# A transformer layer on eight cores: new assumed delays, banks, buffers and places of small work in a statically scheduled kernel

## Chip, cores, metric

One Trainium2 chip, all eight cores running the same program on different tokens. The time is device microseconds of the slowest core. Fast runs are compared with fast runs; a run in which one die shows a lower granted tensor-engine clock is left out (2058.0 us in one run of the changed kernel, with cores 0 to 3 at 0.825 to 0.838 and the others at 0.997).

## The reference, cut

```python
def hybrid_layer(x, c, ...):                       # x (1, 8192, 2048), c (1, 2048), f32
    mod = jax.nn.silu(c) @ w_ada + b_ada           # six vectors of 2048: conditioning
    shift_m, scale_m, gate_m, shift_f, scale_f, gate_f = split(mod, 6)
    h = rms_norm(x, g_pre_mix) * (1.0 + scale_m) + shift_m
    u, v, p, ga, gb = split(h @ w_in, ...)         # 2048, 2048, 1024, 2048, 2048 columns
    y_a = spatial_gating(gelu(u), gelu(v), ...) @ w_branch_a
    y_b = multiscale_pool(p, w_pool, pool_scale) @ w_branch_b
    merged = sigmoid(ga) * y_a + sigmoid(gb) * y_b
    x = x + gate_m * rms_norm(merged @ w_out, g_post_mix)
    h = rms_norm(x, g_pre_ffn) * (1.0 + scale_f) + shift_f
    a, g = split(causal_depthwise_conv(h @ w_up, conv_w, conv_b), 2)   # 2 x 5632
    return x + gate_f * rms_norm((gelu(a) * g) @ w_down, g_post_ffn)
```

Each core handles 1024 tokens plus a halo, feature-major, mostly in float16 with float32 PSUM.

## The kernel before, where the change touches it

The kernel records every operation, then orders each engine's queue at build time with a cost model. The queues are written in that order, so a wrong cost becomes a wrong place in a queue.

```python
# the model's idea of when an operation ends
if o.dma:
    free[e] = t + (1100.0 if e == "pool" else 80.0)
    pipe = max(pipe, t + 1000.0) + o.cost          # bytes / 335, in ns
    o.end = pipe + 1200.0
else:
    free[e] = t + o.cost
    o.end = t + o.cost + o.lat
...
def dot(self, out, in0, in1, accum, soon):         # one conditioning value per partition, on DVE
    ...
    if soon:
        o.at = self.npe + 60                       # due 60 matmuls from here
```

The conditioning vectors are dot products on the vector engine, of 128 weight rows at a time, streamed through small buffers beside other work:

```python
mtile = [view(SC, i * 4096, 4096, H16, 1) for i in range(3)]
def mod_next(upto, ntile):
    while mdone[0] < upto:
        while mdone[0] - mdone[1] >= ntile:
            mod_dot_next()                         # frees a buffer: POOL's next load waits for it
        ...
        S.dma("pool", t[:, 0, :], w_adaT[r:r + 128, :], writes=[t])
...
def g_step():                                      # once per pair of gate-stage weight tiles
    g_next()                                       # next 1 MB of w_gab
    npairs[0] += 1
    n = npairs[0]
    mod_next(3 + n * 3 // 2 if n <= 12 else min(len(mf), n + 9), 3 if n <= 12 else 1)
    if n in (19, 21):
        load("o%d" % (n // 20), (RD, n // 20 * 16384), *specs["o%d" % (n // 20)])
```

The start of branch B, where the last pooling blocks are evicted:

```python
for eb, at in ((0, y0), (1, 3072)):
    S.act(qv[6 + eb][:, 0:1024], ps[:, at:at + 1024], AF.Identity, scale=col(vec, V_PS + eb))
...
state["slot"] += 1                                 # output block 1 takes the banks of block 0
yb_mms(0, b0, range(6, 8))
```

The second norm reads residual rows through six buffers while w_up is being loaded:

```python
xs2 = [...2 in SC...] + [...4 in RC...]
for j in {9: (1, 2), 11: (0, 3), 15: (4,)}.get(i, ()):
    load_up((0, 0, j), PL[j])
```

## Time and profile before

| | before |
|---|---|
| median of the 5 runs | 1787.31 us (1784.23 to 1817.48) |
| spans of the cores in the profiled run | 1772.0 to 1784.7 us |
| tensor engine busy, slowest core | 1682.8 us, 94% |
| waits of the tensor engine after its first main matmul, mean of the cores | 24.9 us |
| stretches at half clock between there and the end, mean per core (20 of the 22 last 3.41 us, two last 6.83) | 2.8 |
| after the last matmul | 13.9 us |

PE stands for the matmuls of the tensor engine, PEld for its weight loads, DVE for the vector engine, ACT for the scalar engine; POOL and SP issue the loads. w_gab are the weights of the gate stage. An eviction copies a result out of a PSUM bank; a matmul that takes the same bank waits for it (1.27 us at 159.7 us on core 3 of the kernel before). "First main matmul" is the 241st of the tensor engine, the first of the pooling projection, at about 80 us. A row of the waits view names the engine that sat idle, whose result ended the wait, the total, the number of waits and the longest. A timeline row gives start, duration, engine, operation and tiles, and in brackets the idle time before it and what ended it. Almost every compute row has one of a few source lines, those of the helpers that record it, so one goes by the tiles: in SC<-SC,xlo 128x1152 a weight tile is multiplied with the conditioning vector in xlo.

### The profile page before, as it was taken

What the parts mean: (1) busy time and instruction counts of PE and PEld (TensorE: products, weight loads), DVE (VectorE), ACT (ScalarE), POOL (GpSimd) and SP (SyncE); (2) the same over time, 40 slices, a digit from 0 to 9 for tenths busy, and PEclk for the clock granted to TensorE, in tenths of its full rate; (3) what the DMA queues carried; (4) which work ended last, traced back from release to release, by engine and by line L of the source; (5) the groups of instructions that cost most, each with busy time, mean ns of one, the idle gap of its engine ahead of it and who ended that gap; (6) DMA issues with size and microseconds to landing.
All of it is one profiled execution on the core that took longest, in us unless ns stands there. A gap on an engine that the chain in (4) does not pass through costs nothing.

```text
span 1784.7 us, 32368 instructions; the slowest of 8 cores (1772.0 to 1784.7 us)
## 1 busy us (share of the span) xinstructions
PE 1682.8 (94%) x12892; PEld 1226.1 (69%) x12892; DVE 1186.0 (66%) x1664; ACT 663.6 (37%) x980; POOL 125.9 (7%) x194
## 2 busy tenths in 40 slices
PE   4399999999999999999989999999999999999996
PEld 1265544566788888877568885588854887488876
DVE  0566614464778668750667998467987678967968
ACT  5115522511233332122768542255410442035475
POOL 0100100000011010100000000000000000100100
PEclk9999999999999999999999999999999999999998
DMA  9998999933799976994797544545435553555496
GB/s 247 165 169 145 150 170 153 151 66 62 123 164 157 159 133 128 150 164 67 184 213 169 97 84 71 95 84 95 83 59 97 94 88 53 98 95 95 68 226 227
DMA packets 85160, 227.42 MB, mean 127 GB/s; under 512 B 5650, under 2 KB 34706, under 8 KB 84499
## 3 DMA queue, kind: packets, MB, share of 16 engines
q0 software_dynamic: 54368, 178.79, 60.6%
q1 hardware_dynamic: 30644, 46.56, 8.6%
q8 instruction: 104, 1.70, 0.4%
q14 instruction: 44, 0.36, 0.1%
HBM read 387.34 MB, written 16.78 MB: 226 GB/s over the span
## 4 chain that ended last, share of the span: by engine, by line
PE 68%; DMA 19%; DVE 7%; issue 3%; ACT 1%; SPq 1%; POOL 0%; DVEq 0%; ACTq 0%; POOLq 0%
PE ps L311 68%; DMA R<-w_adaT 5%; DMA SC<-w_adaT 5%; DMA RING<-w_adaT 3%; DMA RD<-w_sA 2%; DVE R L340 2%; DMA RC<-xT 1%; DMA R<-xT 1%; DVE R L323 1%; DVE SC L335 1%; DVE RING L340 1%; DMA RING<-w_down 1%; SPq L355 1%; DVE SC L340 1%; DVE SC L323 1%
## 5 line engine op out<-in xcount | busy, mean ns | idle before, releaser
L311 PE MATMUL ps<-RD,RING 128*128 128x257 f16 (+2 forms) x5172 | 654.0, 283 | 7.0 <-ACT SC L318 3.1
L311 PEld LDWEIGHTS ps<-RD,RING 128*128 128x128 f16 x5172 | 504.0, 98 | 128.6 <-issue 9.4
L318 ACT ACTIVATE R<-ps 128x514 f32<-128x514 f32 (+4 forms) x222 | 140.3, 633 | 563.5 <-PE ps L311 544.0
L311 PE MATMUL ps<-RC,RING 128*128 128x257 f16 (+6 forms) x2168 | 347.1, 313 | 0.3 <-DMA RING<-w_down 0.2
L311 PEld LDWEIGHTS ps<-RC,RING 128*128 128x128 f16 x2168 | 207.4, 98 | 118.0 <-issue 1.9
L335 DVE SCALAR_TENSOR_TENSOR SC<-SC,vec 128x1024 f32<-128x1024 f32 (+1 forms) x188 | 218.3, 1178 | 14.1 <-ACT SC L318 7.6
L323 DVE TENSOR_TENSOR RING<-RING 128x1024 f16<-128x1024 f16 (+2 forms) x250 | 157.7, 640 | 26.5 <-PE ps L311 18.8
L323 DVE TENSOR_TENSOR SC<-ps,R 128x514 f32<-128x514 f32 x144 | 99.5, 691 | 88.3 <-PE ps L311 75.9
L311 PE MATMUL ps<-RING 128*128 128x257 f16 x1248 | 146.5, 274 | 0.0
L323 DVE TENSOR_TENSOR R<-ps,R 128x512 f32<-128x512 f32 (+4 forms) x174 | 104.4, 613 | 46.3 <-PE ps L311 44.2
L311 PEld LDWEIGHTS ps<-RING 128*128 128x128 f16 x1248 | 122.1, 98 | 18.0
L311 PE MATMUL ps<-SC,RING 128*128 128x342 f16 (+1 forms) x654 | 125.5, 341 | 5.6 <-ACT RC L318 3.7
L311 PE MATMUL ps<-RING,RD 128*128 128x512 f16 x576 | 125.1, 379 | 1.3 <-ACT R L318 0.7
L318 ACT ACTIVATE SC<-SC,vec 128x1024 f32<-128x1024 f32 (+1 forms) x94 | 108.4, 1158 | 38.8 <-DVE SC L323 27.8
L318 ACT ACTIVATE SC<-ps 128x514 f32<-128x514 f32 (+1 forms) x89 | 55.8, 627 | 137.8 <-PE ps L311 137.6
L311 PEld LDWEIGHTS ps<-SC,RING 128*128 128x128 f16 x654 | 63.9, 98 | 59.3 <-issue 8.6
L311 PEld LDWEIGHTS ps<-RING,RD 128*128 128x128 f16 x576 | 56.2, 98 | 69.6 <-issue 2.2
L311 PE MATMUL ps<-R 128*128 128x257 f16 x816 | 96.5, 274 | 2.7 <-DVE SC L323 2.7
L311 PE MATMUL ps<-R,RING 128*128 128x257 f16 x816 | 96.2, 274 | 1.2 <-ACT R L318 0.8
L318 ACT ACTIVATE RD<-ps 128x514 f32<-128x514 f32 (+2 forms) x77 | 45.7, 593 | 123.5 <-PE ps L311 123.4
L311 PEld LDWEIGHTS ps<-R 128*128 128x128 f16 x816 | 79.8, 98 | 14.9 <-issue 3.4
L311 PEld LDWEIGHTS ps<-R,RING 128*128 128x128 f16 x816 | 79.5, 98 | 13.2 <-issue 1.7
(142 smaller groups left out, 1454.8 us busy)
## 6 DMA issues: line engine op xcount, KB each, us to landing
RING<-w_up POOLq DMA_DIRECT2D x44, 1024.0 KB, 8.0
RING<-w_gab POOLq DMA_DIRECT2D x24, 1024.0 KB, 9.7
SC<-w_adaT POOLq DMA_DIRECT2D x32, 512.0 KB, 11.8
RING<-w_in POOLq DMA_DIRECT2D x7, 2048.0 KB, 22.5
R<-w_adaT POOLq DMA_DIRECT2D x6, 2048.0 KB, 18.9
RING<-w_down POOLq DMA_DIRECT2D x16, 768.0 KB, 6.7
RING<-w_down POOLq DMA_DIRECT2D x14, 640.0 KB, 6.2
R<-xT SPq DMA_DIRECT2D x15, 576.0 KB, 16.4
```

The costliest lines, as they stand in the source:

```text
L311: return self.op("pe", lambda e: e.matmul(out, lhsT=lhsT, rhs=rhs, start=start, stop=stop, skip_group_check=resume), [lhsT, rhs], [out], s ...
L318: return self.op("act", lambda e: e.activation(out=out, in_=in_, func=func, bias=bias, scale=scale, accum_out=accum), self._aps(in_, scale ...
L323: return self.op(eng, lambda e: e.tensor_tensor(out=out, in0=in0, in1=in1, op=op), [in0, in1], [out], cost=65.0 + per * self._n(out))
L335: return self.op("dve", lambda e: e.scalar_tensor_tensor(out=out, in0=in0, scalar=s, in1=in1, op0=op0, op1=op1), self._aps(in0, s, in1), [ ...
L340: o = self.op("dve", lambda e: e.scalar_tensor_tensor(out=out, in0=in0, scalar=1.0, in1=in1, op0=ALU.mult, op1=ALU.mult, accum_out=accum), ...
L355: return self.op(eng, lambda e: e.dma_start(out=out, in_=in_), reads, writes, rtags, wtags, dma=True, cost=b / 335.0, after=after)
```

## The change

The intent: keep the tensor engine fed. The cost model gets an assumed lag for loads that arrive late and a later deadline for the dots; several blocks get other banks or buffers; eight of 32 conditioning tiles move to the output projection; projection blocks cover evictions; and the tail handles several blocks per instruction. The core of the diff, with cuts marked:

```diff
-                o.end = pipe + 1200.0
+                o.end = pipe + 1200.0 + o.lat
...
-            o.at = self.npe + 60
+            o.at = self.npe + soon                 # 60, and 180 for the gate stage's dots
...
 # lags: shift loads 2000, gm3 30000, gate-stage tiles 5000 (1000 for gf), second norm's residuals 3000
-            load("gm%d" % g, (R1, 16512), *specs["gm%d" % g])
+            load("gm%d" % g, (R1, 16512), *specs["gm%d" % g], lag=30000.0 if g == 3 else 0.0)
...
 # pairs of pooling blocks: the second trails by two steps
-            for kc in kcs:
-                fm_mms(b0, p_w(n), h_rhs, PCS_P, [kc], kcs[-1] + 1, kcs[0])
-                fm_mms(b1, p_w(n + 1), h_rhs, PCS_P, [kc], kcs[-1] + 1, kcs[0])
+            for i in range(len(kcs) + 2):
+                fm_mms(b0, p_w(n), h_rhs, PCS_P, kcs[i:i + 1], kcs[-1] + 1, kcs[0])
+                fm_mms(b1, p_w(n + 1), h_rhs, PCS_P, kcs[i - 2:i - 1] if i > 1 else (), kcs[-1] + 1, kcs[0])
...
-        for eb, at in ((0, y0), (1, 3072)):
-            S.act(qv[6 + eb][:, 0:1024], ps[:, at:at + 1024], AF.Identity, scale=col(vec, V_PS + eb))
         for eb in range(2):
             S.act(qv[6 + eb][:, 1024:1026], rest[...], ...)
-        state["slot"] += 1
+        for a in (0, 512):
+            S.act(qv[6][:, a:a + 512], ps[:, y0 + a:y0 + a + 512], AF.Identity, scale=col(vec, V_PS))
+            S.ts(qv[7][:, a:a + 512], ps[:, 3072 + a:3584 + a], col(vec, V_PS + 1), ALU.mult)
...
-                    for c in range(8):
+                    for c in (0, 1, 2, 6, 7, 3, 4, 5):
...
+        MG = 24
-            mod_next(3 + n * 3 // 2 if n <= 12 else min(len(mf), n + 9), 3 if n <= 12 else 1)
-            if n in (19, 21):
-                load("o%d" % (n // 20), ...)
+            mod_next(3 + n * 3 // 2 if n <= 12 else min(MG, n + 9), 3 if n <= 12 else 1)
+            if 18 <= n < 22:
+                i = (n - 18) // 2
+                load("o%d" % i, (RD, i * 16384), *specs["o%d" % i], 4, only=[n % 2 * 2, n % 2 * 2 + 1])
...
-        mod_next(3, 3)
-            g_plain("gb", QH, i // 4, i % 2, 1 - i // 2 % 2, (0, 2, 4)[i % 3])
+            g_plain("gb", QH, i // 4, i % 2, 1 - i // 2 % 2, (4, 0, 4, 2)[i])
...
-        g_pairs(gq[17:], QU, lambda: None)
+        g_pairs(gq[17:], QU, lambda: ox.append(out_cover()))   # 14 k-steps of output block 0
         ...
+        out_part(1, 2 - ox[0], range(14))
...
+        xs2 = 15 residual buffers instead of 6
-            for j in {9: (1, 2), 11: (0, 3), 15: (4,)}.get(i, ()):
+            for j in {9: (1,), 11: (0, 3)}.get(i, ()):          # j = 4 and 2 after the second norm
...
 # output projection, first half
+            if i % 2 == 0:
+                mod_next(MG + 1 + i // 2, 2)
...
 # first up blocks: 14 k-steps of two or three blocks interleaved, other banks
-                plain((1, 2, 0, 3, 4), 0, (0, 3, 6), False, ...)
+                plain((1, 0, 3, 4, 2), 0, (6, 3, 0), False, ...)
...
 # tail: blocks per eviction in the four token sets
+        groups = [[1] * 16, [2] * 8, [2] * 8, [4, 4, 4, 2, 2]]
```

More of the change, by code (lines that the diff above doesn't have):

```diff
@@ L351, in memset, with dma @@
         return self.op(eng, lambda e: e.memset(out, v), [], [out], cost=60.0 + 0.3 * self._n(out))
-    def dma(self, eng, out, in_, reads=(), writes=(), rtags=(), wtags=(), after=()):
+    def dma(self, eng, out, in_, reads=(), writes=(), rtags=(), wtags=(), after=(), lag=0.0):
         b = int(np.prod(in_.shape)) * (4 if in_.dtype == F32 else 2)
         return self.op(eng, lambda e: e.dma_start(out=out, in_=in_), reads, writes, rtags, wtags, dma=True, cost=b / 335.0,
-                       after=after)
+                       lat=lag, after=after)
 def build_program():
@@ L438, in piece_dst, with load @@
             return view(where[0], where[1], nk * ncols * 2, H16, nk)
-        def load(key, where, w, r0, nk, c0, ncols, parts=1, only=None, after=()):
+        def load(key, where, w, r0, nk, c0, ncols, parts=1, only=None, after=(), lag=0.0):
             dst = piece_dst(where, nk, ncols)
@@ L455, in load @@
                     src = w[(r0 + i * n) * 128:(r0 + (i + 1) * n) * 128, c0:c0 + ncols].rearrange("(k p) n -> p k n", p=128)
-                last = S.dma("pool", d, src, writes=[d], after=after)
+                last = S.dma("pool", d, src, writes=[d], after=after, lag=lag)
             loaded[key] = dst
@@ L498, in like, with rsqrt @@
             return v3(ap2, len(pieces))
-        def rsqrt(out, in_, scale):
-            S.act(out, in_, AF.Ln, scale=scale, bias=epst[:])
+        def rsqrt(out, in_, scale, table=True):
+            o = S.act(out, in_, AF.Ln, scale=scale, bias=epst[:])
+            if not table:
+                o.cost -= 1300.0
             S.act(out, out, AF.Exp, scale=-0.5)
@@ L519, in mod_c, with mod_dots @@
             return d
-        def mod_dots(key, f0, acc=None, soon=True):
+        def mod_dots(key, f0, acc=None, soon=60):
             w = loaded[key]
@@ L715, in shift_load @@
         def shift_load(i, after=()):
-            load("h%d" % i, (RING, 16384 + i % 3 * 4096), *specs["h%d" % i], after=after)
+            load("h%d" % i, (RING, 16384 + i % 3 * 4096), *specs["h%d" % i], after=after, lag=2000.0)
         def shift_add(i):
@@ L721, in shift_add @@
             o, sh = hT[:, i, :], mod_fm[:, i:i + 1]
-            S.tt(sh, col(macc, i), col(bada, i), ALU.add)
+            d = S.tt(sh, col(macc, i), col(bada, i), ALU.add)
             if i == 15:
                 S.stt(o, o, sh, ALU.add, xlo[:], ALU.add)
-            else:
-                S.act(o, xres[i], AF.Identity, scale=col(gs_m, i), bias=sh)
+            elif i % 2 == 0:
+                S.ts(o, xres[i], col(gs_m, i), ALU.mult, sh, ALU.add)
+            if i % 2 == 0 and i:
+                S.act(hT[:, i - 1, :], xres[i - 1], AF.Identity, scale=col(gs_m, i - 1), bias=mod_fm[:, i - 1:i], after=[d])
         for n in range(4, 8):
@@ L766, in build_program @@
                     shift_step(i)
-                load_next(0)
+                    if i == 6:
+                        load_next(0)
         load_next(2)
@@ L867, in build_program @@
         gst = [view(SC, 12304 + i * 2056, 2056, F32) for i in range(2)]
-        macc2 = view(SC, 16416, 128, F32)
+        macc2 = view(SC, 16528, 128, F32)
         merged = yb
@@ L891, in mod_dot_next @@
             mdone[1] += 1
-            mod_dots("%s.%d" % (sec, f), f, macc2 if sec == "gf" else None)
+            mod_dots("%s.%d" % (sec, f), f, macc2 if sec == "gf" else None, 180)
             if (sec, f) == ("sf", 15):
@@ L907, in mod_next @@
                 r = ((("hf", "sf", "gf").index(sec) + 2) * 16 + f) * 128
-                S.dma("pool", t[:, 0, :], w_adaT[r:r + 128, :], writes=[t])
+                S.dma("pool", t[:, 0, :], w_adaT[r:r + 128, :], writes=[t], lag=5000.0 if sec != "gf" else 1000.0)
                 loaded["%s.%d" % (sec, f)] = t
@@ L1013, in g_step @@
             n = npairs[0]
-            mod_next(3 + n * 3 // 2 if n <= 12 else min(len(mf), n + 9), 3 if n <= 12 else 1)
-            if n in (19, 21):
-                load("o%d" % (n // 20), (RD, n // 20 * 16384), *specs["o%d" % (n // 20)])
+            mod_next(3 + n * 3 // 2 if n <= 12 else min(MG, n + 9), 3 if n <= 12 else 1)
+            if 18 <= n < 22:
+                i = (n - 18) // 2
+                load("o%d" % i, (RD, i * 16384), *specs["o%d" % i], 4, only=[n % 2 * 2, n % 2 * 2 + 1])
         for i in range(3):
@@ L1030, in build_program, with out_cover, out_part @@
         g_step()
+        while mdone[1] < MG:
+            mod_dot_next()
         g_token_sums(QU)
-        g_pairs(gq[17:], QU, lambda: None)
-        while mdone[1] < len(mf):
-            mod_dot_next()
+        def out_cover():
+            x = 2 * (ng[0] % 2)
+            out_part(0, x, range(14))
+            return x
+        def out_part(blk, b0, kcs):
+            for kc in kcs:
+                for pi, (c0, n) in enumerate(PCS_1):
+                    S.mm(bank(b0 + pi)[:, 0:n], loaded["o0"][:, kc, blk * 128:(blk + 1) * 128], merged[:, kc, c0:c0 + n], kc == 0, kc == KC - 1)
+        ox = []
+        g_pairs(gq[17:], QU, lambda: ox.append(out_cover()))
         load("o2", (RING, 0), *specs["o2"])
         load("o3", (RING, 16384), *specs["o3"])
+        out_part(1, 2 - ox[0], range(14))
         mixT = view(R1, 0, 65664, F32, 16)
@@ L1041, in build_program, with out_block @@
         sqx = [view(R1, 65664 + i * 1156, 1156, BF16) for i in range(3)] + [view(RD, 32896, 1156, BF16)]
-        def out_block(blk, pieces):
+        def out_block(blk, pieces, b0=None):
             w = loaded["o%d" % (blk // 4)]
             c0, n = pieces[0][0], sum(m for _, m in pieces)
-            pv = fm_block(lambda kc: w[:, kc, (blk % 4) * 128:(blk % 4 + 1) * 128], lambda kc, a, m: merged[:, kc, a:a + m], pieces)
+            if b0 is not None:
+                out_part(blk, b0, range(14 if blk < 2 else 0, KC))
+                pv = bview(b0, pieces)
+            else:
+                pv = fm_block(lambda kc: w[:, kc, (blk % 4) * 128:(blk % 4 + 1) * 128], lambda kc, a, m: merged[:, kc, a:a + m], pieces)
             i = state["rr"] % len(sqm[n])
@@ L1056, in sum_mms, with rms @@
                 S.mm(bank(b0 + pi)[:, 0:n], ones_bf[:], sq[:, c0 - pieces[0][0]:c0 - pieces[0][0] + n], first, last, side=True)
-        def rms(b0, dst, pieces):
-            rsqrt(like(dst, pieces), bview(b0, pieces), 1.0 / D)
+        def rms(b0, dst, pieces, table=True):
+            rsqrt(like(dst, pieces), bview(b0, pieces), 1.0 / D, table)
         rs1, rs2 = view(SC, 0, 2312, F32), view(SC, 8224, 1792, F32)
@@ L1063, in build_program @@
         xs1 = [view(RING, 32768 + 2312 * i, 2312, F32) for i in range(7)] + [view(SC, 10016 + 2312 * i, 2312, F32) for i in range(2)]
-        xs2 = [view(SC, 10016 + 2312 * i, 1792, F32) for i in range(2)] + [view(RC, 24576 + 1792 * i, 1792, F32) for i in range(4)]
+        xs2 = ([view(SC, 10016 + 2312 * i, 1792, F32) for i in range(2)] + [view(SC, 14640, 1792, F32)] +
+               [view(RING, 40992 + 1792 * i, 1792, F32) for i in range(4)] + [view(RC, 24576 + 1792 * i, 1792, F32) for i in range(4)] +
+               [view(RING, 24576 + 1792 * i, 1792, F32) for i in range(4)])
         def norms(pieces, rs, xs, b0):
@@ L1071, in norms @@
                 m, x = mixT[:, i, c0:c0 + n], xs[i % len(xs)]
-                S.dma("sp", x, xT[i * 128:(i + 1) * 128, 126 + c0:126 + c0 + n], writes=[x])
+                S.dma("sp", x, xT[i * 128:(i + 1) * 128, 126 + c0:126 + c0 + n], writes=[x], lag=3000.0 if c0 else 0.0)
                 S.tt(m, m, rs, ALU.mult)
@@ L1138, in build_program @@
         fq += [("dn", (3, j)) for j in range(3)]
-        for i, blk in enumerate(range(16)):
-            sum_mms(6, out_block(blk, PCS_1), PCS_1, i == 0, i == 15)
+        state["slot"] = 0
+        for i in range(16):
+            sum_mms(6, out_block(i, PCS_1, (ox[0], 2 - ox[0], 4)[i] if i < 3 else None), PCS_1, i == 0, i == 15)
+            if i % 2 == 0:
+                mod_next(MG + 1 + i // 2, 2)
+        while mdone[1] < len(mf):
+            mod_dot_next()
         rms(6, rs1, PCS_1)
@@ L1239, in plain, with mms @@
             todo = [(j, m) for j in js for m in range(2)]
-            if t:
-                first = bufs[:3]
-                for kc in range(KC):
-                    for i, (j, m) in enumerate(todo[:3]):
-                        for pi in range(2):
-                            S.mm(bank(first[i] + pi)[:, 0:257], loaded[("up", 0, 0, j)][:, m, kc, :],
-                                 h2T[:, kc, t, pi * 257:(pi + 1) * 257], kc == 0, kc == KC - 1)
+            def mms(b0, j, m, kcs):
+                for kc in kcs:
+                    for pi in range(2):
+                        S.mm(bank(b0 + pi)[:, 0:257], loaded[("up", 0, 0, j)][:, m, kc, :],
+                             h2T[:, kc, t, pi * 257:(pi + 1) * 257], kc == 0, kc == KC - 1)
+            for kc in range(14):
+                for i, (j, m) in enumerate(todo[:2 + t]):
+                    mms(bufs[i], j, m, [kc])
             for i, (j, m) in enumerate(todo):
                 b0 = bufs[i % len(bufs)]
-                if not t or i > 2:
-                    for kc in range(KC):
-                        for pi in range(2):
-                            S.mm(bank(b0 + pi)[:, 0:257], loaded[("up", 0, 0, j)][:, m, kc, :],
-                                 h2T[:, kc, t, pi * 257:(pi + 1) * 257], kc == 0, kc == KC - 1)
+                mms(b0, j, m, range(14 if i < 2 + t else 0, KC))
                 n = nplain[0]
@@ L1350, in build_program, with last_mms @@
         SETS = [(0, 384), (384, 256), (640, 256), (896, 128)]
-        def last_mms(b, o, c0, n, kcs):
+        def last_mms(b, o, c0, n, kcs, at=0):
             w = loaded[("dn", 3, o // 2)]
             for kc in kcs:
-                S.mm(bank(b)[:, 0:n], w[:, o % 2, kc, :], actv[:, kc, c0:c0 + n], kc == 0, kc == NB[3] - 1)
+                S.mm(bank(b)[:, at:at + n], w[:, o % 2, kc, :], actv[:, kc, c0:c0 + n], kc == 0, kc == NB[3] - 1)
         for k in range(NG):
@@ L1360, in build_program @@
                 behind_sq = norms(PCS_2, rs2, xs2, 5)
-                behind_h2 = h2(PCS_2, rs2, xs2)
-                plain((1, 2, 0, 3, 4), 0, (0, 3, 6), False, [behind_h2], [behind_sq])
+                behind_h2 = h2(PCS_2, rs2, xs2[:3] + xs2[7:11])
+                for j in (4, 2):
+                    load_up((0, 0, j), PL[j])
+                plain((1, 0, 3, 4, 2), 0, (6, 3, 0), False, [behind_h2], [behind_sq])
                 ffn_next()
@@ L1366, in build_program @@
                     load("gf%d" % (i + 2), (R1, i * 16384), *specs["gf%d" % (i + 2)])
-                plain(range(5), 1, (6, 2, 4, 0), True)
+                plain(range(5), 1, (4, 2, 0, 6), True)
                 for i in range(2):
@@ L1397, in build_program @@
         rsy = [view(RC, 30720, 1536, F32), view(RD, 35840, 1024, F32), view(RC, 30720, 1024, F32), view(RC, 31744, 512, F32)]
-        sqy = [view(R1, 65536 + i * 768, 768, BF16) for i in range(5)]
+        sqy = [view(R1, 65536 + i * 1024, 1024, BF16) for i in range(4)]
+        groups = [[1] * 16, [2] * 8, [2] * 8, [4, 4, 4, 2, 2]]
         batch = [2, 4, 4, 4]
@@ L1418, in build_program @@
                 last_mms(tb[o], o, c0, n, range(NB[3] - 4 if o < 2 else 0, NB[3] - 2))
-            for o in range(16):
+            o = 0
+            for g in groups[t]:
                 b = tb[state["tm"] % 6]
                 state["tm"] += 1
-                last_mms(b, o, c0, n, range(NB[3] - 2, NB[3]) if o < ahead else range(NB[3]))
-                y = yT[:, o, c0:c0 + n]
-                S.tt(y, bank(b)[:, 0:n], y, ALU.add)
-                sq = sqy[nsq % 5][:, 0:n]
-                nsq += 1
-                S.act(sq, y, AF.Square)
-                sum_mms(sb, sq, [(c0, n)], o == 0, o == 15)
-                S.act(y, y, AF.Identity, scale=col(ggf, o))
-            rms(sb, rsy[t], [(c0, n)])
+                for i in range(g):
+                    last_mms(b, o + i, c0, n, range(NB[3] - 2, NB[3]) if o < ahead else range(NB[3]), i * n)
+                y = yT[:, o:o + g, c0:c0 + n]
+                S.tt(y, v3(bank(b)[:, 0:g * n], g), y, ALU.add)
+                sq = sqy[nsq % 4][:, 0:g * n]
+                nsq += 1
+                S.act(v3(sq, g), y, AF.Square)
+                for i in range(g):
+                    sum_mms(sb, sq[:, i * n:(i + 1) * n], [(c0, n)], o + i == 0, o + i == 15)
+                    S.act(yT[:, o + i, c0:c0 + n], yT[:, o + i, c0:c0 + n], AF.Identity, scale=col(ggf, o + i))
+                o += g
+            rms(sb, rsy[t], [(c0, n)], t == 0)
             if t == 1:
```

## The prediction

> **What bounds the kernel now.** I read the head of the page first, then the cores, then the busy time in stretches of 20 us, then the waits of the tensor engine, and last the timeline at its longest waits.
>
> The page of the slowest core:
>
> ```profile
> span 1784.7 us, 32368 instructions; the slowest of 8 cores (1772.0 to 1784.7 us)
> PE 1682.8 (94%) x12892; PEld 1226.1 (69%) x12892; DVE 1186.0 (66%) x1664; ACT 663.6 (37%) x980; POOL 125.9 (7%) x194
> ```
>
> The tensor engine is busy 94% of the span, so at most about 100 us can be won by filling its holes. The stretches say where they are (columns: stretch, then busy us of PE, PEld, DVE, ACT, POOL with counts, granted clock, DMA share, GB/s):
>
> ```profile
> 40.00:60.00 20.00, 2.22 (x79) 2.20 (x80) 16.68 (x14) 3.10 (x3) 1.42 (x3) 1.00 1.00 157
> 160.00:180.00 20.00, 19.01 (x119) 12.21 (x120) 10.41 (x13) 10.02 (x9) 2.11 (x4) 0.91 1.03 173
> 600.00:620.00 20.00, 20.00 (x181) 17.52 (x179) 13.43 (x22) 7.79 (x13) 3.05 (x5) 1.00 0.85 142
> 740.00:760.00 20.00, 17.60 (x157) 14.96 (x156) 14.92 (x26) 3.21 (x6) 2.42 (x3) 1.00 1.06 184
> 800.00:820.00 20.00, 20.00 (x163) 15.68 (x161) 0.00 (x0) 6.43 (x10) 0.00 (x0) 1.00 1.15 172
> 920.00:940.00 20.00, 15.71 (x133) 12.32 (x131) 15.22 (x28) 11.49 (x20) 0.00 (x0) 1.00 1.03 287
> 1760.00:1780.00 20.00, 9.69 (x165) 9.22 (x162) 17.87 (x34) 10.57 (x39) 0.00 (x0) 0.81 0.47 156
> ```
>
> From 40 to 80 us the engine waits for the scale weights (DMA share 1.00); nothing of the change is there. In 600 to 620 it issues 181 matmuls of mostly 257 columns in 20.00 us, 110 ns each[...]. Adding 20.00 minus PE busy over all stretches from 80 to 1760 gives 30.4 us; the last sum waits 1.15 us more, and 13.9 us run after the last matmul ends. That is all the change can reach. Adding the idle intervals on each core after its first main matmul gives 27.1, 22.7, 24.2, 30.7, 21.0, 23.5, 27.6 and 22.1 us for cores 0 to 7: the slow cores are slow mainly because they have more of these waits.
>
> Who ends them, and two of the longest:
>
> ```profile
> PE ps L311 <- ACT SC L318: 26.5, 25, 9.2
> PE ps L311 <- ACT R L318: 8.0, 8, 1.9
> PE ps L311 <- DVE SC L323: 3.9, 5, 2.0
> PE ps L311 <- DVE R L331: 2.7, 1, 2.7
> PE ps L311 <- DVE RC L323: 1.9, 1, 1.9
> ```
>
> ```profile
> 752.38 1.36 DVE L340 SCALAR_TENSOR_TENSOR SC<-SC,xlo 128x1152 f16<-128x1152 f16 x1 [0.52 <-DMA SC<-w_adaT]
> 753.66 1.09 DVE L340 SCALAR_TENSOR_TENSOR SC<-SC,R 128x896 f16<-128x896 f16 x1
> 754.68 0.69 DVE L323 TENSOR_TENSOR SC<-ps,R 128x514 f32<-128x514 f32 x1
> 755.51 1.94 PE L311 MATMUL ps<-R 128*128 128x257 f16 x16 [2.04 <-DVE SC L323]
> ...
> 927.26 0.63 DVE L323 TENSOR_TENSOR R<-R,RC 128x448 f32<-128x448 f32 x1 [2.54 <-DMA RC<-xT]
> 927.98 0.58 ACT L318 ACTIVATE R<-R 128x448 bf16<-128x448 f32 x1 [2.05 <-DVE R L323]
> 928.70 0.35 PE L311 MATMUL ps<-R,ones_bf 128*128 128x448 bf16 x1 [1.90 <-ACT R L318]
> ```
>
> At 752 the vector engine waits for a late conditioning tile, does its dot product (1.36 + 1.09 us), and only then evicts the bank that the tensor engine wants. At 927 a norm sum was put into the PE queue before its residual had landed. Most of these are errors of static order, made at build time from a cost model that thinks the DMA is earlier than it is.
>
> [...]the clock record of this core has two stretches of 3.413 us at 0.5 after the start, at 161 us (the 0.91 above is 1 - 0.5 x 3.41 / 20) and at 359 us, right behind its waits there; the other cores have two to four. Each costs about 1.7 us, which no wait list shows. [...]block 1 takes the banks of block 0 and waits 1.27 us for ACT. [...]the chain of waits shows one xT load of 21.02 us from 908.63, beside 1 MB w_up loads.
>
> **The change part by part.** Matmul work stays the same; no part makes a matmul cheaper. The whole gain is waits, given as idle on core 3 before, and what I expect to be left.
>
> Pooling projection (95 to 115 us): waits of 0.43, 0.45, 0.94, 0.41 = 2.23. Letting the second block of a pair trail by two steps ends the first 6 matmuls x 0.147 = 0.88 us sooner, so its ACT eviction is done when the next pair wants the bank. Left 0.8.
>
> Pool blocks and start of branch B (146 to 161): 1.10 of small waits, bound by ACT evicting 1.05 us per 0.88 us block, untouched; then 0.93 + 0.41 + 1.27 = 2.6. The two 1024-wide ACT evictions become 512-wide halves shared by ACT and DVE, and the dropped slot step gives block 1 free banks (the 1.27). Left 1.1 + 0.4.
>
> Branch B (194 to 200): 2.43 here, 0 to 0.9 elsewhere; ACT stood behind a shift whose dot was late. Half of the shifts go to DVE, the rest one step later, with 2 us of assumed lag. Left 0.3.
>
> V start: 0.62 + 0.70; the new column order uses the last-evicted banks last, which is worth the 0.62. Left 0.7.
>
> V to U (357): 2.73 for the normalised v (L331), which DVE did after four dots of 9.27 us on the last gate tile. An assumed lag of 30 us puts it ahead of them. Left 0.2.
>
> U to gates (468, 485): 1.62 + 0.84. The 0.84 is a bank reused too soon, mended by the order 4, 0, 4, 2; the 1.62 is a vector queue of dots, only partly touched. Left 0.4.
>
> Gate products (505 to 770): 1.17 + 3.03, mostly dots ahead of evictions. Their deadline goes from 60 to 180 matmuls and their loads get 5 us of lag, and eight of 32 tiles leave this stage. Left 0.8.
>
> Gates to output projection: 0.84 + 1.94. Fourteen k-steps of output block 0 (28 x 0.123 = 3.4 us) now cover the reuse of the bank, fourteen of block 1 the final DVE chain. Left 0.3. The eight moved tiles cost 8 x (1.36 + 1.09) = 19.6 us of DVE, in a stage of 68 us where DVE is at 0.00: hidden.
>
> Norm (918 to 931): 4.90. Seven instead of two residual tiles are loaded ahead and two of five w_up loads go later. Left 1.5.
>
> First up blocks 1.92, left 0.8; FFN 0.87, left 0.7; last sum 1.15, left 0.6.
>
> Sum before 30.7, after 8.6: 22.1 us. Clock drops: 2 x 1.7 = 3.4, I leave 0.9: 2.5 us.
>
> Tail, 13.9 us after the last matmul. DVE runs without a hole to about 1780.3, of which four 1.2 us multiplies are backlog of the set before. Grouping saves DVE 16 x 0.42 - 8 x 0.69 = 1.2 us in each of two sets and 16 x 0.29 - (3 x 0.69 + 2 x 0.42) = 1.7 in the last, 4 us in all (0.69 is the 514-wide PSUM add). Some meets holes DVE has anyway: I take 2.4 us.
>
> Total for core 3: 22.1 + 2.5 + 2.4 = 27.0, so 1757.7. The same left-overs (8.6 + 0.9, tail 2.4) on the others give 1757.0 for core 0, 1758.4 for core 5 (23.5 idle, two drops), 1758.5 for core 6 and 1753 to 1756 for the rest. The slowest is then 1758.5; the run's time was 1.6 over its slowest span and the median 1.0 over that run: 1761. I add 3 us for new waits that a reshuffled order brings on one of eight cores: 1764.
>
> **The rivals.** First, the moved dots take the place of the removed wait: the first norm writes its factor over the tiles' buffers, so a late last dot would hold the norm. Against it: DMA is nearly idle from 820 to 860 us (share 0.00)[...]. If it happens, still 51 us of second-half output matmuls hide it; 0 to 5 us lost, 1764 to 1769. Second, the up weights come too late: block pair j=2 now shares its place with residual tiles and is asked for after the norm has read them, for use 8 blocks x 3.55 us after 907, about 936 to 939. My estimate of its landing is 935 to 938, so 0 to 4 us, 1764 to 1768. Third, the waits are DMA jitter that no static lag cures: then only the structural ones go (about 13 us with one clock drop) and it is about 1773. For it speaks that idle differs between cores running one program; against it, that most of those differences sit at a dot or a norm sum, which now has slack. Fourth, everything is filled: 1784.7 - 30.7 - 3.4 = 1750.6 before the tail, and 1751 as a time.
>
> **Range and chances.** 2% is 35.7 us, to 1751.6: nearly every wait and most of the spare tail would have to go, 0.05. Slower than 1823 needs a new stall larger than all the old ones, 0.02; within 2%, 0.93. The range is 1756 (nearly the plain sum, a lucky slowest core) to 1775 (jitter).
>
> **What would show it.** PE busy 20.00 in 720 to 780 and from about 900 to 940; no clock below 1.00 between 100 and 1700; no wait on L331 near 357 nor on DVE RC before the output projection; w_adaT dots on DVE inside the output projection; less than 12 us after the last matmul; a smaller spread of cores than 12.7 us. I am wrong if PE idle after 80 us stays above 18 us on the slowest core, if a wait on w_up or on SC appears around 855 to 940, or if busy matmul time itself changes.

The passages cut stated rules and figures that no run of this case shows. No term of the sum is among them: it comes to 1764 us as it stands. That a busy matmul is at its limit is among them and was the author's estimate; what was measured is that the matmuls were busy for 1682.8 us before and 1677.0 us changed on the slowest cores. The block 1 that waits 1.27 us is that of the branch-B output, at 159.7 us.

## The result

| | before | changed |
|---|---|---|
| median of all runs of that comparison, slow ones included | 1787.16 us | 1759.29 us |
| spans of the cores, profiled runs | 1772.0 to 1784.7 us | 1750.5 to 1757.8 us |
| from the first main matmul to the end, mean of the cores | 1698.4 us | 1673.9 us |
| waits in it, mean (range) | 24.9 (21.0 to 30.7) us | 8.2 (6.4 to 10.6) us |
| half-clock stretches that begin in it, per core | 2 to 4 | 0 |
| after the last matmul | 13.85 us | 12.56 us |

The ratio is 0.9841 (95% interval 0.9825 to 0.9856). A ratio is the mean time of one kernel's fast runs over that of the other's of the same rounds, so it is not quite the ratio of the medians. It is faster, clear of noise, by 1.6%, so within 2%. The result is correct.

The head of the page of the changed kernel, then its cores 0 to 3:

```profile
span 1757.8 us, 32263 instructions; the slowest of 8 cores (1750.5 to 1757.8 us)
PE 1677.0 (95%) x12892; PEld 1225.7 (70%) x12892; DVE 1192.6 (68%) x1647; ACT 648.6 (37%) x945; POOL 130.5 (7%) x200
```

```profile
core 0: 1756.9 us, clock 0.997
core 1: 1751.3 us, clock 0.997
core 2: 1757.8 us, clock 0.983
core 3: 1751.9 us, clock 0.997
```

The 12892 matmuls are the same and their busy sum moved by 6 us only; what went is the time between. In each pair 0/1, 2/3, 4/5, 6/7 one core is about 6 us later than the other; which one changes from run to run. (The low clock mean of core 2 comes from a half-clock stretch at the start, from 35.3 us on, while it waits for weights. It lasts to 86.5 us, 6 us into the main matmuls, and costs this core an estimated 3 us, half of those 6.)

The stretches of the changed kernel that answer to those in the prediction:

```profile
160.00:180.00 20.00, 20.00 (x139) 13.29 (x137) 12.87 (x15) 8.62 (x8) 2.18 (x5) 1.00 1.03 172
740.00:760.00 20.00, 20.00 (x181) 17.49 (x180) 13.77 (x24) 3.13 (x6) 0.00 (x0) 1.00 0.55 133
800.00:820.00 20.00, 20.00 (x163) 15.68 (x161) 9.52 (x16) 5.71 (x10) 2.12 (x4) 1.00 0.71 126
920.00:940.00 20.00, 20.00 (x182) 17.53 (x180) 13.69 (x24) 19.40 (x30) 1.48 (x2) 1.00 1.03 194
```

PE is at 20.00 in all four, and the clock at 1.00. In 160 to 180 it now issues 139 matmuls where it issued 119. The moved dots are seen in 800 to 820: DVE went from 0.00 to 9.52 us there, and the matmuls are still 163. What is left to wait for in the middle of the program (waits of the tensor engine, changed kernel, its slowest core):

```profile
PE ps L311 <- ACT R L318: 3.1, 5, 1.2
PE ps L311 <- DVE SC L335: 2.2, 3, 1.1
PE ps L311 <- DVE RD L329: 2.0, 2, 1.6
PE ps L311 <- DMA RING<-w_gab: 1.4, 1, 1.4
```

The rows of L331 and of DVE RC are gone, that of ACT R fell from 8.0 to 3.1. The L331 wait is a good one to read in the timeline. Before, core 3:

```profile
346.28 1.23 DVE L340 SCALAR_TENSOR_TENSOR R<-R,SC 128x1024 f16<-128x1024 f16 x1 [16.26 <-DMA R<-w_adaT]
347.39 0.19 ACT L318 ACTIVATION_READ_ACCUMULATOR R<-R 128x1 f32 x1
359.08 3.71 DVE L331 TENSOR_SCALAR R<-R,vstat 128x2048 f16<-128x2048 f16 x5 [1.71 <-ACT vstat L318]
360.04 0.27 PE L311 MATMUL ps<-SC,R 128*128 128x128 f16 x1 [2.73 <-DVE R L331]
```

Changed, core 0:

```profile
342.00 6.59 DVE L331 TENSOR_SCALAR R<-R,vstat 128x2048 f16<-128x2048 f16 x9 [2.09 <-ACT vstat L318]
344.37 0.22 PE L311 MATMUL ps<-SC,R 128*128 128x128 f16 x1
```

Before, DVE stood idle for 16.26 us because the next item of its queue was the dot of a gate tile that had not landed. Once it had, 9.27 us of dots came first. The normalisation of v, whose last statistic was ready at 347.58 us, stood behind them until 355.5. So it was the dots that held the tensor engine, not the idle time itself, which ended before the statistics were there; an earlier landing would have hidden them in it. Changed, DVE normalises first, and the first spatial-gating matmul has no wait.

Where the 24.5 us from the first main matmul on went: waits 24.9 - 8.2 = 16.7; half-clock stretches, 24 times 3.41 us on eight cores or 3.0 per core x 1.7 us = 5.1; the tail 1.3; together 23.1. The rest is hidden in the waits: from start to start the 2.73 us wait costs 2.89 us, a 1.62 us one 1.78, so these two cost 0.16 us more than their brackets say. There are 13.6 fewer waits per core (29.4 before, 15.8 changed); at 0.16 us each that is an estimated 2.2 us: the sum closes to within 1 us.

### The profile page after: what moved, and what is told of

The parts are those of the page before. It is cut to its first block, busy times and chain, and to the rows that moved or that the text cites. A ratio compares the mean times of both kernels' runs of the same rounds, so it can differ in the third digit from the quotient of the medians.

```text
span 1757.8 us, 32263 instructions; the slowest of 8 cores (1750.5 to 1757.8 us)
## 1 busy us (share of the span) xinstructions
PE 1677.0 (95%) x12892; PEld 1225.7 (70%) x12892; DVE 1192.6 (68%) x1647; ACT 648.6 (37%) x945; POOL 130.5 (7%) x200
## 4 chain that ended last, share of the span: by engine, by line
PE 83%; DMA 8%; DVE 5%; issue 2%; SPq 1%; ACT 1%; POOL 0%; DVEq 0%; ACTq 0%; POOLq 0%
PE ps L311 83%; DMA RING<-w_gab 3%; DMA RD<-w_sA 2%; DVE RC L323 1%; DMA R<-xT 1%; DMA RING<-w_adaT 1%; DVE R L323 1%; DVE SC L335 1%; DMA RING<-w_down 1%; SPq L356 1%; DVE RING L340 0%; ACT SC L318 0%; DVE RC L335 0%; DVE SC L323 0%; DVE RD L329 0%
## 5 line engine op out<-in xcount | busy, mean ns | idle before, releaser
L323 DVE TENSOR_TENSOR R<-ps,R 128x512 f32<-128x512 f32 (+2 forms) x147 | 100.8, 698 | 48.7 <-PE ps L311 46.3
```

The lines of the kernel that those rows point to most:

```text
L323: return self.op(eng, lambda e: e.tensor_tensor(out=out, in0=in0, in1=in1, op=op), [in0, in1], [out], cost=65.0 + per * self._n(out))
```

## Experiments

Twelve runs, on three chips. Each part is judged by where its waits stand, and by the mean time from the first main matmul to the end ("post-start") over cores whose clock was undisturbed. That leaves out the start, which moves by about 2 us from profile to profile. It is 1698.4 us before and 1673.9 changed. The changed kernel repeats this on two of them (1673.4 and 1673.7, see Control). The kernel before was profiled once only, so differences against 1698.4 are less certain: gm3_only shows by how much. Of the pieces in the diff, five groups were taken out alone (cost model, start of branch B, tiles, norm, tail). The two-step trail of the pooling pairs, the shifts on DVE, the new orders of columns and banks and the 14 k-steps that cover evictions were tested only together, in structure_only.

**The order alone.** Kernel before, with the numbers of the cost model only:

```diff
+ lags on the late loads, dots due after 180 matmuls in the gate stage, gm3 30 us late, one table load not counted
  (no instruction, bank or buffer differs)
```

> The kernel before with only the numbers of the build-time cost model changed (assumed lag of late loads, deadline of the dots 180 matmuls instead of 60, the assumed lag of 30 us on the last gate tile, the table load left out of one cost); no instruction and no buffer differs, only the order of issue. Theory (the order was wrong because DMA was assumed too early): the wait near 357 us on the normalised v disappears on all cores (1.3 us on average, 3.0 on core 0), the waits of branch B (0.7) and about half of the gate stage waits (3.9 in the three parts) too, and one clock drop of 1.7 us on the cores that had one there: 5 to 9 us on the slowest core, so 1778 to 1782. The structural waits (1.27 us at the start of branch B, 0.84 us on reused banks, the output projection) must stay. Rival (DMA jitter that no fixed order cures, or only the new buffers and banks count): within 2 us of 1787.

Measured: fast runs 1773.3 to 1775.3 us, correct; the ratio on that chip is 0.9959 (0.9932 to 0.9987) with three of six runs slow and a wide scatter of the kernel before, so I go by the trace: post-start 1687.8, that is 10.6 us less. The wait before the first U block is 0.00 on all eight cores (mean 1.29 before), branch B 0.00 (0.68), the gate stage with its start 2.7 (5.4). The structural waits, those of banks and buffers that this version leaves alone, stayed as expected: start of branch B 2.82, output projection 0.84, norm 2.9. The order also brought new waits: 3.0 us in the first up blocks where the kernel before had 1.5 (one of 1.5 to 1.6 us on all eight cores), and 1.05 on w_gab instead of 0.23. The times are under the 1778 to 1782 expected, but the kernel before was faster on this chip too (five of its six fast runs 1778.5 to 1785.8). Jitter falls as the main cause: most waits that differ between cores are cured by a fixed order, though not those on w_gab.

**The structure alone.** The changed kernel with the old cost model (the table load is counted again, too).

```diff
-                o.end = pipe + 1200.0 + o.lat
+                o.end = pipe + 1200.0
-            o.at = self.npe + soon
+            o.at = self.npe + 60
```

> The changed kernel with the old cost model: no assumed lags, dots due after 60 matmuls, the table load counted. Buffers, banks, splits, moved tiles and grouped tail stay. Theory: it loses what the order alone gives, the wait of up to 3 us before the first U block comes back on some cores, with its clock drop, and a few dots stand ahead of evictions in the gate stage: 1764 to 1769. If order_only and this one add up, their two gains sum to about 28 us. Rival (order is worth nothing once the structure is there): 1758 to 1761.

Measured 1766.8 to 1773.3 us, post-start 1682.3, or 16.1 us less than before. Order 10.6 and structure 16.1 sum to 26.7 against 24.5 together: nearly additive, as far as the one profile of the kernel before can say, which stands in all three numbers. The wait before the first U block is not merely back, it averages 4.4 us where the kernel before had 1.3. Core 1 of this run:

```profile
341.92 1.23 DVE L340 SCALAR_TENSOR_TENSOR R<-R,SC 128x1024 f16<-128x1024 f16 x1 [16.60 <-DMA R<-w_adaT]
355.51 0.27 PE L311 MATMUL ps<-SC,R 128*128 128x128 f16 x1 [7.71 <-DVE R L331]
```

The tensor engine reaches this point about 10 us earlier than core 3 of the kernel before (at 347.8 instead of 357.3), which fits the waits ahead of it being gone, while the gate tile lands only 4 us earlier: part of what the structure won is given back at the next mis-ordered queue.

**One lag alone.** Kernel before, only the gate tile's lag:

```diff
+load("gm%d" % g, (R1, 16512), *specs["gm%d" % g], lag=30000.0 if g == 3 else 0.0)
```

> The kernel before with one number changed: the last gate tile is assumed 30 us later at build time. Theory (one vector queue order is the whole cause of the wait before the first U block): mean wait there 0.0 instead of 1.3 us, no drop at 359 us, all other waits as before, so 2 us less on average from the first main matmul to the end, 1696, and 3 to 5 us on cores that had it. Rival (the wait needs the other order changes as well): still 1 us or more there on some cores.

Measured: that wait is 0.00 on all cores, and no clock drop at 359 us; one fast run, 1779.6 us, which says nothing by itself; post-start 1694.1. The one number is the whole cause of that wait. It explains only 1.7 of the 4.3 us: 1.29 of wait and two stretches in eight cores. The other 2.6 us are fewer waits and stretches elsewhere; whether chance, the chip or a queue order that shifted with the number made them was not separated. A difference of this size against the one profile of the kernel before says little by itself.

**The slot step.**

```diff
+        state["slot"] += 1
         yb_mms(0, b0, range(6, 8))
```

> The changed kernel with the one dropped slot step put back, so that block 1 of branch B takes the banks of block 0 again. Theory (the wait of 1.27 us near 160 us is that, and together with its neighbours it trips the clock drop that all eight cores of the kernel before show at 157 to 161 us): wait back; if the drop returns too, 3.0 us slower than the changed kernel, 1762; if the wait alone is too short to trip it, 1.3 us slower, 1760.5. Rival (the tensor engine catches up later, since DMA bounds this stage): no difference, 1759.3.

Measured 1758.6 to 1760.1 us. The wait is back at exactly 1.27 us on all eight cores (1.62 with its 0.35 neighbour); no clock drop. Post-start 1675.9, 2.0 us more, of which 0.9 is a larger wait at the start of the gates. The end-to-end time does not show it: in this profile the first main matmul comes 1.5 us earlier, in the mean of the cores, than in that of the changed kernel, which was taken at another time.

**The whole start of branch B as before.** Also the two 1024-wide ACT evictions, ahead of the small ones. The three waits meant, in the kernel before (core 3):

```profile
158.11 0.60 PE L311 MATMUL ps<-SC,RING 128*128 128x342 f16 x3 [0.93 <-ACT SC L318]
159.12 0.60 PE L311 MATMUL ps<-SC,RING 128*128 128x342 f16 x3 [0.41 <-ACT SC L318]
160.99 1.23 PE L311 MATMUL ps<-SC,RING 128*128 128x342 f16 x5 [1.27 <-ACT RC L318]
```

```diff
-        for a in (0, 512):
-            S.act(qv[6][:, a:a + 512], ...)
-            S.ts(qv[7][:, a:a + 512], ...)
+        for eb, at in ((0, y0), (1, 3072)):
+            S.act(qv[6 + eb][:, 0:1024], ps[:, at:at + 1024], ...)
+        state["slot"] += 1
```

> The changed kernel with the whole start of branch B as before: two 1024-wide ACT evictions, the small ones last, and the slot step. Slot_skip gave back the 1.27 us but no clock drop. Theory ([...]0.93 + 0.41 + 1.27 within 3.8 us did): 2.6 us of waits and the drop near 157 us on all undisturbed cores, together 4 us from the first main matmul to the end, 1677.5. Rival (the drop of before came from the earlier waits of the projection too): waits back, no drop, 1675.8.

Measured: one fast run, 1761.7 us, beside 1757.5 for the changed kernel on that chip; waits 2.60 on every core, post-start 1678.0, 4.1 us more; the half-clock stretch on cores 0, 1, 4 and 7. Two cores with exactly the same busy time show what a drop costs, core 1 and then core 2 (stretch 150 to 170 us):

```profile
150.00:170.00 20.00, 17.41 (x106) 10.22 (x105) 11.14 (x14) 7.66 (x9) 2.83 (x5) 0.91 1.03 167
```

```profile
150.00:170.00 20.00, 17.41 (x117) 10.70 (x116) 11.68 (x17) 8.56 (x10) 2.96 (x5) 1.00 1.04 176
```

Both wait 2.6 us. At clock 0.91 the one issues 106 matmuls, at 1.00 the other 117. The eleven missing ones, at 342 columns (147 ns from start to start on average, core 2 of the changed kernel, 155 to 200 us), are 1.6 us. So 1.27 us of idle did not trip it on any core (slot_skip), and 2.6 us within 4 us did on four of eight here. The same 2.6 us did on all eight cores in the profile of the kernel before and on five of eight in gm3_only, which has the same waits in the projection as well: these do not decide it. Nor does one threshold. Over all fourteen kept profiles, the shortest single wait with a stretch behind it is 1.99 us (kernel before, core 5 at 781 us), while one of 2.94 us has none (gm3_only, core 6 at 773 us). What decides between 2 and 3 us was not found.

**The eight tiles back in the gate stage.**

```diff
-        MG = 24
+        MG = 32
 # and the loads and dots of the last eight out of the output projection
```

> The changed kernel with the eight moved conditioning tiles back in the gate stage, and nothing of them in the output projection. Theory (their dots ahead of evictions, and their loads beside w_gab, made the waits of 2.5 us from 740 to 780 and part of the 1.9 us before the output projection): 3 to 5 us slower than the changed kernel, 1762 to 1764, with idle near 740 to 785 us of 2 us or more. Rival (the later deadline of the dots alone cured them): 1759 to 1760 and no idle there.

Measured 1764.5 to 1764.8 us, ratio 0.9906 (0.9884 to 0.9927), post-start 1679.1: 5.2 us more. The idle is there, 4.1 us on average, with a clock drop on every core, but it is not what I expected to see. The longest, core 6:

```profile
751.58 6.37 PE L311 MATMUL ps<-R,RING 128*128 128x257 f16 x32 [5.88 <-DMA RING<-w_gab]
```

It waits for weights, not for an eviction behind a dot. With the later deadline no wait for an eviction is left there, but POOL holds the next loads until a dot has freed the single tile buffer (12.6 us in one place), and the tiles share the DMA with w_gab, w_out and the residuals (share 1.10 and 1.06 from 720 to 760 us). In this version it is the loads that moving the tiles relieves.

**The second norm as before.**

```diff
-        xs2 = 15 buffers; j = 4 and 2 loaded after the norm
+        xs2 = 6 buffers; {9: (1, 2), 11: (0, 3), 15: (4,)}
```

> The changed kernel with the second norm as before: six residual tiles instead of fifteen, and the w_up loads of j=2 and j=4 issued early again. Theory (the 4.1 us of waits near 925 us were residual loads queued behind w_up, which the assumed lag alone cannot cure: order_only still shows 2.9 us there): 2 to 4 us of idle back at 905 to 940 us, a clock drop on some cores, 1762 to 1765. Rival (the assumed lag of 3 us on the residual loads did it, by placing the norm sums later in the queue): idle stays near 0.2 us and 1759 to 1760.

Measured on a chip where one or two pairs of cores ran at a lower clock in many runs; the one undisturbed run took 1765.2 us. On the six undisturbed cores of the profile post-start is 1681.2, over 7 us more; the norm waits are back at 4.0 us instead of 0.20, the first up blocks at 2.3 instead of 0.97, and five of the six cores have a half-clock stretch. Core 4:

```profile
907.33 0.62 DVE L323 TENSOR_TENSOR R<-R,RC 128x448 f32<-128x448 f32 x1 [3.29 <-DMA RC<-xT]
908.77 0.53 PE L311 MATMUL ps<-R,ones_bf 128*128 128x448 bf16 x1 [3.35 <-ACT R L318]
```

The assumed lag is still in this version and does not help; structure_only, without the lag, waits 0.20. It was the buffers and the loads. Which of those two counts more was not separated. (Start of branch B, tiles and norm, put back one at a time, cost 4.1 + 5.2 + 7.3 = 16.6 us, more than the 13.9 between order_only and the changed kernel: the parts are not independent. The wait of 1.51 us in the first up blocks here, for one, is as in order_only and comes with the old norm under the new order.)

**The tail one block at a time**, with the five smaller buffers for squares that go with it.

```diff
-groups = [[1] * 16, [2] * 8, [2] * 8, [4, 4, 4, 2, 2]]
+groups = [[1] * 16] * 4
```

> The changed kernel with the tail handled one output block at a time again. Theory of the prediction (DVE backlog sets the tail): the tail after the last matmul returns from 12.6 to about 13.3 to 13.9 us, 0.7 to 1.3 us in time; the last sum waits 0.9 to 1.2 us. Order_only, which has the old grouping and the new cost of the table load, shows 13.3. Rival (tail is set by the store's own latency alone): 12.6 us still, no difference.

Measured 1757.1 to 1758.8 us in fast runs: no slower than the changed kernel within the scatter of chips, and the control of this chip has no undisturbed run. Post-start is 1674.0, beside 1673.4 on the control's six undisturbed cores. The tail is 13.34 us instead of 12.56, but the last sum waits 0.94 instead of 1.33, since it need not wait for a group. Grouping is worth 0.4 us, less than the 0.7 to 1.3 expected; another 0.5 us of tail (13.85 to 13.3) comes with the cost-model numbers alone.

**Control.**

> The changed kernel, unaltered, as the control of this chip. Its time on record is 1759.3 us, mean span 1754.2 us, with mean idle of the tensor engine after the start of 8.2 us and no clock drop. Expected: 1758 to 1761 with the same idle. The time until the first main matmul differs from run to run by up to 2 us, so the parts are compared by the span after it as well.

> The changed kernel unaltered, the control for the version below. Expected 1757 to 1760 in undisturbed runs, 1673.4 to 1673.9 us from the first main matmul to the end as a mean over undisturbed cores.

Measured on the second chip: 1779.1 to 1779.8 us; in each of these runs one pair of cores had a mean clock of 0.98. In the profiled one cores 4 and 5 did, and took 1772.8 and 1778.2 us (the clock record of core 4 stands at 0.8125 for 160 us, from 88 us on); the other six cores give 1673.4 post-start and the same waits part by part. On the third chip: 1756.8 to 1759.0 us, ratio 0.9866 (0.9840 to 0.9892), post-start 1673.7.

**An attempt at something better.** On the later core of each pair, w_gab lands late near 520 us (waits of 0.9 to 1.7 us on cores 0, 2, 4 and 7 of the changed kernel), with conditioning tiles loaded beside it. First:

```diff
-            mod_next(3 + n * 3 // 2 if n <= 12 else min(MG, n + 9), 3 if n <= 12 else 1)
+            mod_next(min(MG, 1 + n * 3 // 2), 3 if n <= 14 else 1)
```

> The changed kernel with two conditioning tiles less in flight at the start of the gate stage (1 + 1.5 per step instead of 3 + 1.5 per step; the same 24 by the sixteenth step). Theory (what is left on the slower core of each pair is w_gab landing late behind 512 KB tiles: 0.9 to 1.7 us near 520 us on cores 0, 2, 4, 7 of the profile): that wait goes, 1 us less on the slowest core, 1758 to 1758.5. Rival (the slower core is late because of its partner, not because of the tiles): the wait stays and 1759.3.

Wrong result (relative error 0.41): with three buffers in use after step 12, the sigmoids of blocks 12 to 15 are written over tiles whose dots come later. This is my reading of the edit; that the version below, with three buffers only up to step 12, is correct bears it out. Mended:

```diff
+            mod_next(1 + n * 3 // 2 if n <= 12 else min(MG, n + 7), 3 if n <= 12 else 1)
```

> The failed version mended: 1 + 1.5 conditioning tiles per step with three buffers only up to the twelfth step, then one per step through one buffer, so that no tile lies where the late sigmoids are written; the result must be correct. The failed one showed no wait at all on w_gab in the first gate products (0.00 instead of 0.3 to 0.7 us on average) and 1756.6 us. Theory: 0.5 to 1.5 us faster than the control, with those waits at 0. Rival: the last five tiles, one per step, bring a wait near 700 us instead, and it is the same as the control.

Correct, and the same: fast runs 1756.6 to 1758.1 us beside 1756.8 to 1759.0 for the control, both at ratio 0.9866. The waits on w_gab are 0.00 on all cores (0.41 in the control), but those in the channel mixer rose from 0.99 to 1.66 on average, 4.96 on core 6:

```profile
PE ps L311 <- DMA RING<-w_down: 3.3, 3, 1.7
```

In these two runs the later core of a pair then gets its weights late at a later stage. Whether the partner is the reason was not shown; running one core of each pair alone was not tried. So no version here beats the changed kernel.

## Why the prediction was right, point by point

The size: 1764 with a range of 1756 to 1775, measured 1759.3. The main step, that the matmul work stays the same and that only the waits, the clock drops and the tail can go, held: the matmul count is the same (12892) and the sum of waits went from 30.7 (core 3) to 6.4 to 10.6, against 8.6 predicted. The slowest span was put at 1758.5 and is 1757.8. The error of 5 us is mostly the last two steps of the sum: the 3 us for new waits of a reshuffled order were not needed, and the 1.0 us from the profiled run to the median was scatter of the kernel before; the changed kernel's fast runs lie within 1.2 us. That the sum of waits came out so close, 8.2 against 8.6, is in part luck: six terms were put too high by 2.5 us in all and six too low by 2.0, and the 0.9 us too many left for the clock offset most of the 1.1 us too much taken off the tail. One reading was wrong without consequence: two of the half-clock stretches (core 1 at 920 us, core 6 at 926) last 6.83 us and cost twice the 1.7 us counted. Of the signs named beforehand one failed: 12.56 us, and not less than 12, pass after the last matmul.

| term, us | core 3 before | left, predicted | left, mean of the cores |
|---|---|---|---|
| pooling projection | 2.23 | 0.8 | 0.56 |
| pool blocks and start of branch B | 3.70 | 1.5 | 1.94 |
| branch B | 2.43 | 0.3 | 0.00 |
| V start | 1.32 | 0.7 | 1.02 |
| V to U | 2.73 | 0.2 | 0.00 |
| U to gates | 2.46 | 0.4 | 0.74 |
| gate products | 4.20 | 0.8 | 0.67 |
| gates to output projection | 2.78 | 0.3 | 0.00 |
| norm | 4.90 | 1.5 | 0.20 |
| first up blocks | 1.92 | 0.8 | 0.97 |
| FFN | 0.87 | 0.7 | 0.73 |
| last sum | 1.15 | 0.6 | 1.33 |
| half-clock stretches | 3.4 | 0.9 | 0.0 |
| taken off the tail | | 2.4 | 1.3 |

Mis-sized terms. **The tail**: grouping was to take off 2.4 us; the tail fell by 1.3, of which tail_old gives grouping 0.8, and 0.4 after what the last sum waits more. The saving met holes. The last four large multiplies are backlog before and after the change. Before:

```profile
1770.90 3.49 DVE L323 TENSOR_TENSOR R<-R,RD 128x1024 f32<-128x1024 f32 x3
1776.12 1.22 DVE L323 TENSOR_TENSOR R<-R,RD 128x1024 f32<-128x1024 f32 x1
```

Changed:

```profile
1733.33 0.69 DVE L323 TENSOR_TENSOR R<-ps,R 128x512 f32<-128x512 f32 x1 [1.65 <-PE ps L311]
1735.78 0.69 DVE L323 TENSOR_TENSOR R<-ps,R 128x512 f32<-128x512 f32 x1 [1.76 <-PE ps L311]
1744.01 3.49 DVE L323 TENSOR_TENSOR R<-R,RD 128x1024 f32<-128x1024 f32 x3
1749.22 1.22 DVE L323 TENSOR_TENSOR R<-R,RD 128x1024 f32<-128x1024 f32 x1
```

A group of four is evicted only when its fourth block is summed, so DVE waits 1.65 and 1.76 us for the tensor engine (core 2), and the three and one multiplies at the end are the same. The **last sum** waits longer, 1.33 and not 0.6; without groups it waits 0.94 (tail_old). **Norm**: too pessimistic; with seven tiles ahead and less w_up traffic only 0.20 is left. **Gate products**: the size was right, but of the two causes I named, the dots ahead of evictions near 750 us go with either cure: order_only, without moved tiles, and structure_only, with the old deadline and no lags, have no such wait there on any core. What the moved tiles do besides is keep POOL's loads from waiting for a dot (12.6 us on core 6 of tiles_back, no such wait from 690 to 760 us on core 0 of the changed kernel) and lighten the DMA where the wait was (share 1.06 in tiles_back, 0.24 changed, core 6 from 740 to 760 us): structure_only has no wait at all between 700 and 800 us. **Clock**: I left half a drop, and none remained; the longest wait left on any core of the changed kernel is 1.72 us (core 4 at 521 us), and the shortest that tripped a drop in any profile is 1.99.

Rivals: no wait appears behind the moved dots (0.00 in the output projection) or on w_up (the load of j=2 landed at 921 to 930 us, 12.2 to 14.9 us after its issue; the 935 to 938 was an estimate that does not say from which numbers); jitter is ruled out as the main cause by order_only; "everything filled" would have been 1751, and 8.2 us of waits are left.

## What to carry to other kernels

In a statically ordered kernel, look for an engine whose written order takes up the work of a late load just when work that others wait for becomes ready behind it: one assumed delay in the cost model took such a wait away on all cores (gm3_only, 1.29 us on average to 0.00), and without it gains made upstream were given back (structure_only, 4.4 us). Size a set of small waits by their sum, and by whether they lie close together, since a cluster of 2.6 us brought a half-clock stretch on four of eight cores, about 1.6 us on the one compared (poolb_old, 106 matmuls on core 1 against 117 on core 2). Judge parts by their own place in the trace and from a fixed early event on: here a 2 us change was invisible end to end.
